# A two-layer hybrid trunk on one core: first stage, latents and side product written in another order, and the delta rule's scratch stored by GpSimd

## The chip, the cores and the metric

The kernel runs on one core of a Trainium2 chip. The time of a run is the device time of that core in microseconds (us). Besides the plain times there is one profiled execution of the kernel, from which all views of the profile come.

## What is computed

Two layers of a trunk over 1024 tokens of width 1024, all in float32. The even layer is a multiscale pool and a differential attention side by side; the odd layer is latent attention (MLA) and a gated delta rule side by side. After each layer a gated side product is added.

```python
def even_layer(h, ...):
    z = h @ w_in
    a_in, a_gate, q, k, v, b_gate = _split(z, EVEN_WIDTHS)
    a = multiscale_pool(a_in)            # trailing-window mean minus the token
    a = (a @ pool_w) * pool_scale * silu(a_gate)
    q, k = partial_rope(rmsnorm(q)), partial_rope(rmsnorm(k))
    o = diff_attention(q, k, v, lam)     # two softmaxes, second one times lam
    o = rmsnorm(o) * silu(b_gate)
    return concat([a, o]) @ w_out

def odd_layer(h, ...):
    cq, ckv, k_rope, c_gate, qkv, d_b, d_a, d_gate = _split(h @ w_in, ODD_WIDTHS)
    q = rmsnorm(cq) @ w_uq;  kv = rmsnorm(ckv) @ w_ukv
    oc = causal_attention(rope(rmsnorm(q)), rope(rmsnorm(k)), v_c) * silu(c_gate)
    dq, dk, dv = silu(causal_depthwise_conv(qkv))
    beta = sigmoid(d_b);  g = -exp(a_log) * softplus(d_a + dt_bias)
    od = gated_delta_rule(l2norm(dq), l2norm(dk), dv, g, beta)   # chunks of 64
    od = rmsnorm(od) * silu(d_gate)
    return concat([oc, od]) @ w_out

for i in range(2):
    h = h + (even_layer, odd_layer)[i](rmsnorm(h, norm_g[i]), ...)
    h = h + sigmoid(h @ ple_w_gate[i]) * (p[i] @ ple_w_proj[i])
```

## The kernel before

**Matrix products.** Every large product is made in float32r with both operands split into a high and a low part, three matmuls for one (`mm3`, L142 to L144). `split` makes the parts: ScalarE copies the high part (L134), VectorE subtracts (L135). `wload` loads 128 rows of a weight into one of four `raw` buffers by a transfer that SP issues (L158), and splits it into one of nine `hi` and nine `lo` slots. `proj_T` makes a transposed block of 128 features by 512 tokens, 24 matmuls at eight rows of weights; `proj_tok` a block of 128 tokens. Results stand in eight PSUM banks: two `acc`, two `s`, two `x`, one `tr`, one `o`.

**Order.** Each engine executes its own list of instructions in order. A scheduling layer makes the lists from the program, so that code written in one order need not stand so on an engine. Larger pieces are Python generators, and `step(...)` advances them one piece at a time, which lays one piece's matmuls beside another's vector work.

**First stage.** The input arrives in two halves of 512 tokens (`load_x`), each split per row block k. The first half makes four column blocks of the pool's input in `first`. The second makes three in `second`, and the fourth (`proj_T`, j = 3) after all k, so that the nine weight slots are held until then. `finish_x` turns the sums of squares into a reciprocal root per token (`token_rstd`, L182; `token_row`, L190). `pool_in` scales the columns to the pool's input (L347, L350, L352). `even_pool(b)` makes window sums by shifted additions on GpSimd (L421), finishes them on VectorE (L431 to L433) and multiplies by `pool_w` (L437). `even_proj` makes a head's q, k, v and gate; its L463 reads a gate from the product's bank.

**Heads and filler.** Six heads of attention follow, `even_attn(hd)` beside `even_proj(hd + 1)`; beside head 5 runs `ple_proj(0)`, the first side product (`pT` times `ple_w_proj`, stored at L595). `out_stage` ends a layer; at the end of layer 0 it sums the squares of its result (L687) for the next normalization.

**Odd layer.** `latent` makes, for each of eight blocks of 128 tokens, a block z (24 matmuls of 456 columns), normalizes it (L771), transposes it (L774) through the one `tr` bank and splits it. `decay` makes the delta rule's gates (L852 to L870). `mla_qkv` makes queries, keys and values per token block, with the weights of `latent_weights` (L788). `gdn_qkv` and `gdn_prep` make, for each of four heads and two halves, six scratch arrays of 128 x 512 and store them to DRAM: q (L899), kw and kd (L952), vb (L957), L and QK (L968). `block_load` reads L back in another layout (L980) and `block_solve` inverts all the diagonal blocks at once on VectorE (L994, L996). `mla_prep` makes K and Q for attention (L1144 to L1146, reading `zq`). `ple_proj(1)` makes the second side product beside that. `gdn_solve` builds the inverse U from the solved blocks (L1010, transposed at L1020 to L1022, matmuls from L1027), then the scan and the MLA attention run beside each other, and `out_stage` ends the layer.

## Time and profile before

| | |
|---|---|
| median of three runs | 1472.44 us (1470.59 to 1477.74) |
| the profiled execution | 1472.82 us |
| its span | 1471.1 us |
| mean clock granted to TensorE | 0.993 of full speed |
| TensorE busy | 1415.7 us, 96% of the span |
| the one queue of transfers (all issued by SP) | 39.7% of what 16 DMA engines could take |

The span is the time from the first to the last recorded instruction. PE is TensorE, DVE VectorE, ACT ScalarE, POOL GpSimd; SP's queue is written SPq. A row of the timeline gives start, duration, engine, line, operation, output and inputs, and in square brackets the idle time of the engine just before it with what ended that. A row of a stretch gives its length and busy time of each engine, then the clock that was granted, the share of the DMA engines and GB/s.

The page's chain of work that ended last holds 3% of TensorE and nothing else of weight; it is the end of `out_stage` of layer 1, which the diff does not touch. So the views that matter are those by stretch and by wait.

### The profile page before, as it was taken

How to read it: one execution, taken by the hardware profiler on the slowest of the kernel's cores; microseconds unless marked ns; L12 is line 12 of the kernel's file. 1: busy time of each engine (PE TensorE's matmuls, PEld its weight loads, DVE VectorE, ACT ScalarE, POOL GpSimd, SP SyncE). 2: the span in 40 equal slices, each digit the busy share in tenths (PEclk: the TensorE clock that was granted, in tenths of full speed). 3: DMA queues.
4: the chain of work that ended last, by engine and by line, in shares of the span. 5: the costliest groups of instructions: out<-in, count | busy, mean ns of one | idle time of the engine just before them, and what ended most of it. 6: DMA issues, size and time to landing. Idle time of an engine off the chain costs nothing. (4 is left out here: it accounts for less than half of the span.)

```text
span 1471.1 us, 22586 instructions
## 1 busy us (share of the span) xinstructions
PE 1415.7 (96%) x7447; PEld 1153.8 (78%) x7447; DVE 977.9 (66%) x2853; ACT 664.6 (45%) x1662; POOL 195.9 (13%) x341
## 2 busy tenths in 40 slices
PE   8999999999999999999999999999989999999998
PEld 6677888888887778887777878778768888887876
DVE  6756766666667785366676788997557887633342
ACT  6335555565656732343554543434334455722220
POOL 0321101111011000022015621210000000000021
PEclk9999999999999999999999999999999999999999
DMA  6223424232333563333424433343676634443332
GB/s 225 61 70 103 108 51 108 51 108 51 101 101 99 160 200 109 108 121 119 103 70 165 181 107 102 99 134 110 214 250 195 204 124 135 129 137 104 126 108 86
DMA packets 127605, 181.51 MB, mean 123 GB/s; under 512 B 28393, under 2 KB 55297, under 8 KB 127489
## 3 DMA queue, kind: packets, MB, share of 16 engines
q1 hardware_dynamic: 127488, 180.08, 39.7%
q8 instruction: 59, 0.97, 0.3%
q14 instruction: 58, 0.47, 0.1%
HBM read 108.20 MB, written 52.95 MB: 110 GB/s over the span
## 5 line engine op out<-in xcount | busy, mean ns | idle before, releaser
L143 PE MATMUL acc<-wl,x 128*128 128x512 f32 (+1 forms) x576 | 229.5, 399 | 3.2 <-DVE wl L135 3.2
L142 PE MATMUL acc<-wh,x 128*128 128x512 f32 (+1 forms) x576 | 231.0, 402 | 0.7 <-DVE g L463 0.6
L144 PE MATMUL acc<-wh,x 128*128 128x512 f32 (+1 forms) x576 | 228.0, 396 | 0.0
L142 PE MATMUL acc<-x,wh 128*128 128x512 f32 x504 | 202.9, 403 | 6.1 <-ACT wh L134 4.6
L144 PE MATMUL acc<-x,wl 128*128 128x512 f32 x504 | 200.2, 399 | 3.6 <-DVE wl L135 3.3
L143 PE MATMUL acc<-x,wh 128*128 128x512 f32 x504 | 199.8, 397 | 0.0
L135 DVE TENSOR_TENSOR wl<-raw,wh 128x512 fp32r<-128x512 f32 (+2 forms) x184 | 124.5, 698 | 31.8 <-ACT wh L134 30.2
L134 ACT CAST wh<-raw 128x512 fp32r<-128x512 f32 (+2 forms) x184 | 105.9, 600 | 69.4 <-PE acc L143 22.6
L143 PEld LDWEIGHTS acc<-wl,x 128*128 128x128 f32 x576 | 109.2, 190 | 26.9 <-DVE wl L135 4.2
L142 PEld LDWEIGHTS acc<-wh,x 128*128 128x128 f32 x576 | 109.2, 190 | 24.4 <-DVE g L463 1.4
L144 PEld LDWEIGHTS acc<-wh,x 128*128 128x128 f32 x576 | 109.0, 189 | 22.5
L142 PEld LDWEIGHTS acc<-x,wh 128*128 128x128 f32 x504 | 94.9, 188 | 29.5 <-ACT wh L134 6.1
L144 PEld LDWEIGHTS acc<-x,wl 128*128 128x128 f32 x504 | 94.8, 188 | 29.5 <-DVE wl L135 7.4
L261 ACT ACTIVATE p<-p,mx 128x128 f32<-128x128 f32 (+7 forms) x128 | 99.4, 777 | 33.7 <-DVE mx L257 23.2
L143 PEld LDWEIGHTS acc<-x,wh 128*128 128x128 f32 x504 | 95.1, 189 | 21.6 <-issue 0.2
L674 POOL TENSOR_TENSOR u<-hp,hp 128x512 f32<-128x512 f32 x32 | 43.2, 1350 | 473.4 <-DVE hp L135 190.8
L144 PE MATMUL acc<-hp,wl 128*128 128x512 f32 x256 | 101.6, 397 | 0.6 <-DVE wl L135 0.6
L143 PE MATMUL acc<-hp,wh 128*128 128x512 f32 x256 | 101.6, 397 | 0.0
L142 PE MATMUL acc<-hp,wh 128*128 128x512 f32 x256 | 101.5, 396 | 0.0
L257 DVE CUSTOM_DVE_ANT_0 p<-s,cst 128x512 f32<-128x512 f32 (+3 forms) x128 | 74.2, 586 | 26.8 <-PE s L532 15.6
L672 DVE SCALAR_TENSOR_TENSOR th<-th,ld 128x512 f32<-128x512 f32 x32 | 30.0, 937 | 75.7 <-ACT th L670 75.7
L459 ACT ACTIVATE z<-acc,rstd 128x256 f32<-128x256 f32 x48 | 22.8, 475 | 101.3 <-PE acc L144 99.1
(554 smaller groups left out, 2866.4 us busy)
## 6 DMA issues: line engine op xcount, KB each, us to landing
raw<-in_ev_w_in SPq DMA_DIRECT2D x56, 256.0 KB
Q<-sq SPq DMA_DIRECT2D x96, 128.0 KB
qkv<-zz SPq DMA_DIRECT2D x16, 640.0 KB
raw<-cat SPq DMA_DIRECT2D x32, 256.0 KB
raw<-in_ple_w_gate SPq DMA_DIRECT2D x32, 256.0 KB
ld<-ple SPq DMA_DIRECT2D x32, 256.0 KB
zq<-qkv SPq DMA_DIRECT2D x16, 512.0 KB
K<-sq SPq DMA_DIRECT2D x48, 128.0 KB
```

What stands on the lines that cost most here:

```text
L134: s.copy(hi, src)
L135: v.tensor_tensor(out=lo, in0=src, in1=hi.bitcast(F32), op=ALU.subtract)
L142: pe.matmul(ps, lh, rh, start=first, stop=False)
L143: pe.matmul(ps, lh, rl, start=False, stop=False)
L144: pe.matmul(ps, ll, rh, start=False, stop=last)
L257: v.tensor_tensor_reduce(out=pm[:, c * 512:c * 512 + n], in0=ps[:, 0:n], in1=mk, scale=-scale, scalar=prev, op0=ALU.add, op1=ALU.min, accu ...
L261: s.activation(pm[:, 0:w], pm[:, 0:w], AF.Exp, bias=prev, scale=-1.0, accum_out=sums)
L459: s.activation(z[:, t % 4, :], ps[:, 0:256], AF.Identity, scale=rstd[0][:, t:t + 1])
L672: v.scalar_tensor_tensor(out=th, in0=th, scalar=1.0, in1=r, op0=ALU.add, op1=ALU.mult)
L674: g.tensor_tensor(out=u, in0=hi.bitcast(F32), in1=lo.bitcast(F32), op=ALU.add)
```

## The change

The change has eight parts.

1. *First stage.* Both halves make all four columns per k (`pool_ps`); the second half has the banks `x`, `x`, `tr`, `o`. Two results of the first half are copied to SBUF by ScalarE, so that the `acc` banks come free. Squares are taken one k behind (`square_x`). `finish_x` uses the banks `acc` and `s`.
2. *Lambda* is made later, after the first step of the pool.
3. *Pool and projection.* `even_pool` is a generator with a pause before its matmuls, and the steps alternate with `even_proj(0)`.
4. *Side product.* `ple_proj` loads the weights of both column halves ahead of its first pause, and head 5 has a longer list of steps.
5. *Sums of layer 0.* The first half's normalization is made after two blocks of the second half.
6. *Latents.* The transposes of a block are written one block later; `latent_weights` is written ahead of the rope, `decay` after two token blocks of `mla_qkv`.
7. *Scratch stores.* The 48 stores of q, kw, kd, vb, L and QK are issued by GpSimd (`g.dma_start`) instead of SP.
8. *`gdn_solve`.* Its copies and negations go from VectorE to ScalarE.

```diff
+    for h in range(2):
+        for k in range(KC):
+            load_x(h, k)
+            if h == 0:
+                w_pool += wload(a["ev_w_in"], 0, 512, row=k, nk=1)
+            if k:
+                square_x(h, k - 1, sums[h])
+            for j in range(4):
+                q = slice(j * P, j * P + P)
+                mm3(pool_ps[h][j], w_pool[k][0][:, q], w_pool[k][1][:, q], *hn[k][h], k == 0, k == KC - 1)
...
-    second.append(bank("acc"))
-    proj_T(hn, w_pool, 3, 1, second[3])
...
+        yield
         for h in range(2):
             pm = bank("s")
             pe.matmul(pm, pw[:, b, :], x[:, 16 + 512 * h:528 + 512 * h], start=True, stop=True)
...
+        w = [wload(a["ple_w_proj"][layer], 512 * gq, 512, nk=2) for gq in range(2)]
         yield
         for gq in range(2):
-            w = wload(a["ple_w_proj"][layer], 512 * gq, 512, nk=2)
...
-    step(ahead)
-    even_pool(0)
-    step(ahead)
-    even_pool(1)
-    step(ahead, ahead)
+    pools_ = [even_pool(b) for b in range(2)]
+    step(pools_[0], ahead)
...
+    step(ahead, pools_[0], pools_[1], ahead, ahead, pools_[1])
...
+        if hd < 5:
+            step(at, at, ahead, late, done, at, at, ahead, at, at, ahead, at, ahead, at, at)
+        else:
+            step(at, at, ahead, ahead, late, done, at, ahead, at, at, ahead, at, ahead, at, ahead, at, ahead, at, ahead)
...
-                if more and gq == 1:
-                    set_rstd(1, h, token_rstd(sums[h]))
+                    if more and gq == h == 1 and j == 1:
+                        set_rstd(1, 0, token_rstd(sums[0]))
+        if more:
+            set_rstd(1, 1, token_rstd(sums[1]))
...
+            zs.append(z)
+            if c:
+                transposes(c - 1)
+        transposes(3)
...
+    we = latent_weights()
     krt = T("gz", 2, pool=bp).rearrange("p (t o d) -> p t o d", o=1, d=64)
     rope(g, kr.unsqueeze(2), krt, cos1, sin1, 1, 32)
-    decay()
-    we = latent_weights()
...
     qkvs, gp0, gp1 = both(), gate_proj(0), gate_proj(1)
-    for _ in range(NT):
+    for t in range(NT):
         step(qkvs, gp0, qkvs)
+        if t == 1:
+            decay()
...
-            dma.dma_start(gsc[n][hd][h], dst)
+            g.dma_start(gsc[n][hd][h], dst)
...
-        v.tensor_copy(W[32:64], ps[32:64, 0:P])
-        v.tensor_copy(W[96:128], ps[96:128, 0:P])
+        s.copy(W[32:64], ps[32:64, 0:P])
+        s.copy(W[96:128], ps[96:128, 0:P])
...
-        v.tensor_scalar(U3[0:64, :, 64:128], c3(px[0:64, 0:256]), -1.0, None, ALU.mult)
+        s.activation(U3[0:64, :, 64:128], c3(px[0:64, 0:256]), AF.Identity, scale=-1.0)
```

Line numbers below that belong to the changed kernel lie about 17 higher than before in the odd layer, and 4 or 5 lower from the even projections to the latents (L463 is L459 there, L774 is L769; L870 is L887, L1027 is L1044).

**VectorE around the end of the first stage.** Before, in this order (`wl` are weights of the products, `Q` and `p` the pool's inputs, `g_785` the gate of the first product block, whose bank the third block needs):

```order
L135 TENSOR_TENSOR wl_779<-raw_777,wh_778 128x512
L207 TENSOR_TENSOR g_628<-g_628 128x64
L212 TENSOR_SCALAR g_628<-g_628 128x64
L431 TENSOR_TENSOR p_847<-p_847,cst 128x16
L433 SCALAR_TENSOR_TENSOR p_180<-p_847,cst,p_180 128x1008
L213 SCALAR_TENSOR_TENSOR pt_629<-g_628 128x64
L432 TENSOR_TENSOR p_180<-p_847,p_180 128x16
L135 TENSOR_TENSOR wl_1228<-raw_1226,wh_1227 128x512
L215 COPY pt_630<-pt_629 128x64
L212 TENSOR_SCALAR g_628<-g_628 128x64
L463 SCALAR_TENSOR_TENSOR g_785<-th_812,acc_786 128x128
```

Now:

```order
L352 TENSOR_TENSOR Q_182<-o_192,g_169 128x512
L203 TENSOR_SCALAR g_630<-cst,npos 128x8 x3
L426 TENSOR_TENSOR p_729<-p_729,cst 128x16
L428 SCALAR_TENSOR_TENSOR p_180<-p_729,cst,p_180 128x1008
L354 SCALAR_TENSOR_TENSOR Q_182<-z_622,Q_182 128x512
L354 SCALAR_TENSOR_TENSOR Q_182<-z_626,Q_182 128x512
L206 TENSOR_SCALAR g_630<-g_630 128x64
L427 TENSOR_TENSOR p_180<-p_729,p_180 128x16
L207 TENSOR_TENSOR g_630<-g_630 128x64
L212 TENSOR_SCALAR g_630<-g_630 128x64
L459 SCALAR_TENSOR_TENSOR g_789<-th_816,acc_790 128x128
```

The weights' splits have left this place for earlier ones. The pool's L426, which reads GpSimd's sums, now stands ahead of both additions into Q and of the gate.

**ScalarE in the first latents.** Before (`z` are latents split out of the transpose bank `tr`, `ea` the decay's exponential, whose `alog` is loaded by SP):

```order
L760 ACTIVATE gz_7844<-acc_7819,rstd_148 128x456
L762 ACTIVATE nx_7845,lss_7847<-gz_7844 128x256
L763 ACTIVATE nx_7845,lss_7847<-gz_7844 128x128
L764 ACTIVATE nx_7845,sskr<-gz_7844 128x64
L134 CAST z_7756<-tr_7809 128x128
L870 ACTIVATE ea_8293<-alog 128x4
L134 CAST z_7757<-tr_7809 128x128
```

Now:

```order
L779 ACTIVATE gz_7836<-acc_7811,rstd_148 128x456
L781 ACTIVATE nx_7837,lss_7839<-gz_7836 128x256
L782 ACTIVATE nx_7837,lss_7839<-gz_7836 128x128
L783 ACTIVATE nx_7837,sskr<-gz_7836 128x64
L134 CAST z_7758<-tr_7861 128x128
L887 ACTIVATE ea_8587<-alog 128x4
L134 CAST z_7759<-tr_7861 128x128
```

The decay is written later in the program, but this operation stands where it stood, between two casts out of the bank.

**SP around the second side product.** Before (`raw` are weights of the second column half, `ple` results, `xinv` the solved blocks, `U` their loads):

```order
L595 DMA ple_3_0_121<-ple_11569 128x512
L158 DMA raw_11588<-in_ple_w_proj 128x512
L595 DMA ple_3_1_122<-ple_11579 128x512
L158 DMA raw_11594<-in_ple_w_proj 128x512
L997 DMA xinv<-nx_11207 128x1024
L1007 DMA L_11805<-gL_0_7660 128x512
L1012 DMA vb_11813<-gvb_0_7652 128x512
L1013 DMA kw_11814<-gkw_0_7636 128x512
L1010 DMA U_11702<-xinv 32x4x32
L595 DMA ple_4_0_123<-ple_11601 128x512
```

Now the four weight loads stand together ahead of the first `zq`, and at this place there is:

```order
L591 DMA ple_3_1_122<-ple_11593 128x512
L1014 DMA xinv<-nx_11233 128x1024
L591 DMA ple_4_0_123<-ple_11603 128x512
L591 DMA ple_4_1_124<-ple_11613 128x512
L591 DMA ple_5_0_125<-ple_11623 128x512
L1027 DMA U_11704<-xinv 32x4x32
L591 DMA ple_5_1_126<-ple_11633 128x512
L1027 DMA U_11704<-xinv 32x4x32
L591 DMA ple_6_0_127<-ple_11643 128x512
L1027 DMA U_11704<-xinv 32x4x32 x2
```

The weight loads are gone from here, and the last two loads of U stand behind the store of the thirteenth result.

## The prediction

> **What bounds the kernel now.** I read the page's list of busy times first, then the busy times of stretches, then what TensorE waited for.

> ```profile
> PE 1415.7 (96%) x7447; PEld 1153.8 (78%) x7447; DVE 977.9 (66%) x2853; ACT 664.6 (45%) x1662; POOL 195.9 (13%) x341
> ...
> core 0: us, PE busy (x) PEld busy (x) DVE busy (x) ACT busy (x) POOL busy (x), PEclk, DMA share, GB/s
> 0.00:100.00 100.00, 89.68 (x365) 69.31 (x366) 71.36 (x180) 44.30 (x80) 20.34 (x39) 0.98 0.35 116
> 440.00:540.00 100.00, 92.08 (x486) 74.20 (x485) 73.98 (x222) 62.04 (x146) 5.46 (x9) 0.98 0.53 163
> 540.00:680.00 140.00, 140.00 (x601) 112.63 (x600) 80.20 (x136) 45.66 (x75) 16.65 (x15) 1.00 0.35 114
> 680.00:800.00 120.00, 111.48 (x514) 91.56 (x513) 80.65 (x305) 57.35 (x201) 28.47 (x63) 0.99 0.35 100
> 840.00:1000.00 160.00, 151.76 (x731) 121.42 (x730) 141.86 (x316) 63.62 (x188) 34.98 (x49) 1.00 0.34 112
> 1040.00:1100.00 60.00, 52.24 (x277) 41.74 (x275) 37.94 (x116) 20.52 (x39) 1.03 (x3) 0.91 0.68 226
> 1100.00:1280.00 180.00, 175.51 (x1537) 152.35 (x1536) 141.99 (x576) 94.81 (x209) 5.04 (x12) 1.00 0.51 156
> ```

> TensorE bounds the whole: it is busy in 1415.7 of 1471.1 us. The change takes no matmul away, so it can win only from the 55.4 us in which TensorE stands still and from the stretches in which its granted clock is below 1.00. The idle time is length less busy time: 10.3 us in the first 100, 7.9 in 440 to 540, 8.5 in 680 to 800, 8.2 in 840 to 1000, 7.8 in 1040 to 1100 and 4.5 in 1100 to 1280. A clock of 0.91 over 60 us is another 5.4 us at most. The stretch 540 to 680 is saturated and gives the price of a 512-column matmul: 140.00 / 601 = 0.233 us.

> ```profile
> PE acc L142 <- ACT wh L134: 8.8, 3, 4.2
> PE acc L143 <- DVE wl L135: 3.2, 1, 3.2
> PE s L1144 <- DMA zq<-qkv: 3.1, 1, 3.1
> PE x L921 <- DVE sp L966: 2.7, 2, 1.5
> PE tr L774 <- DVE z L135: 1.9, 1, 1.9
> PE tr L774 <- DVE gz L771: 1.6, 5, 0.5
> PE x L143 <- DVE nx L135: 1.6, 1, 1.6
> PE o L182 <- DVE sums L687: 1.6, 2, 1.0
> ```

> Columns: total us, times, longest. Each wait is small, so each part of the change is priced at its own wait.

> **First stage, 0 to 100 us.** Timeline rows of four engines (start, us, engine, line; in brackets the idle time before it and what ended it):

> ```profile
> 51.24 2.72 ACT L134 CAST wh<-raw 128x512 fp32r<-128x512 f32 x4 [4.42 <-PE acc L143]
> 58.44 1.92 POOL L421 TENSOR_TENSOR p<-p 128x1039 f32<-128x1039 f32 x1 [28.30 <-DVE p L347]
> 60.62 2.41 POOL L421 TENSOR_TENSOR p<-p 64x1038 f32<-64x1038 f32 x1
> 63.10 2.25 POOL L421 TENSOR_TENSOR p<-Q 128x1039 f32<-128x1039 f32 x1
> 62.01 3.89 DVE L352 SCALAR_TENSOR_TENSOR Q<-z,Q 128x512 f32<-128x512 f32 x2 [0.76 <-ACT z L351]
> 66.85 1.26 DVE L433 SCALAR_TENSOR_TENSOR p<-p,cst,p 128x1008 f32<-128x1008 f32 x1
> 66.66 0.50 PE L143 MATMUL acc<-wl,x 128*128 128x512 f32 x1 [3.15 <-DVE wl L135]
> 68.64 0.63 PE L142 MATMUL acc<-wh,x 128*128 128x512 f32 x1
> 73.44 1.88 PE L437 MATMUL s<-p,pw 128*128 128x512 f32 x4
> ```

> Before, ScalarE waits 4.42 us for TensorE, because all nine weight slots are held until the fourth column of the second half is done. The last splits come late, and one stands behind two VectorE operations that take 3.89 us beside GpSimd's shifted sums. TensorE waits 3.15 us and then runs slow for a while (0.63 us a record where 0.40 is usual; the clock of 0.98 over 100 us bounds that by 2 us, I count 1.7): 4.9 in all. With four columns per k the slots come free with the block, and this goes.

> What is late next: the third product block (acc_859) needs the bank that g_789 (L459) still reads, and g_789 now stands on VectorE behind the pool's L426 and L428. TensorE would be at acc_859 where it now is at 73.44, less 4.9: 68.5. The pool's sums start 19 matmuls later (so many product matmuls stand ahead of the second row product now), 4.4 us, so those that end at 63.0 end at 67.4. From there to g_789 VectorE has L428's 1.26 us, two additions of half its size (0.7 each, an estimate from it) and some 0.8 of small ones: ready at 70.9 alone, or up to 4 later beside GpSimd's next sums (2.25 and more). The wait is 2.4 to 6.4 us; I take 3.5, with 0.8 for half a chance of the slow clock and 0.6 at the next blocks, where the same chain comes round. Against 4.9: **0** (-4 to +3).

> **Filler of head 5, 440 to 540 us.**

> ```profile
> 516.74 0.50 PE L142 MATMUL acc<-x,wh 128*128 128x512 f32 x1 [1.00 <-DVE z L129]
> 520.23 1.02 PE L562 MATMUL tr<-cst,o 128*128 128x128 f32 x4 [0.43 <-DVE o L555]
> ```

> The side product is spread more thinly over head 5, so its weights and the first output products lie between these waits. The two waits are 1.4 us, with their restarts 2; the rope wait and its slow clock at 469 stay. **2** (0 to 5, the upper end all that is not ordinary attention).

> **Latents, 680 to 800 us.** The second half's transposes now stand one block of 24 matmuls behind their z. At 456 columns a block is 24 x 0.208 = 5.0 us (0.233 x 456/512), where the chain needs 18 matmuls and 0.5, 4.2 us: five waits, 1.6 us, go, with 0.4 of restart. The reduction of the first half's sums moves back by more than 30 matmuls, and of L182's 1.6 us about 1.2 go. The decay is written later, but its exponential stands in ScalarE's order where it stood.

> ```profile
> 722.84 0.21 ACT L870 ACTIVATE ea<-alog 128x4 f32<-128x4 f32 x1 [2.60 <-DMA alog<-in_od_a_log]
> ```

> It blocks the casts that free the one transpose bank, so the 1.9 us wait at L774 and its slow clock stay. So does nx at 1.6: rope runs on GpSimd beside it as before. With 0.8 for the decay's other operations: **4** (2 to 7).

> **Scratch stores by GpSimd, 840 to 1000 us.** All 48 stores (q, kw, kd, vb, L, QK; four heads, two halves) leave SP's queue.

> ```profile
> SPq L968 <- DVE sp L966: 40.0, 14, 6.1
> ...
> 922.45 0.32 SPq L968 DMA_DIRECT2D gL<-sp  x1
> 922.86 1.35 SPq L158 DMA_DIRECT2D raw<-in_od_w_in  x3
> 924.63 0.49 ACT L134 CAST wh<-raw 128x384 fp32r<-128x384 f32 x1
> ...
> L674 POOL TENSOR_TENSOR u<-hp,hp 128x512 f32<-128x512 f32 x32 | 43.2, 1350 | 473.4 <-DVE hp L135 190.8
> ```

> Now a store that waits for VectorE holds SP, the next head's weight loads stand behind it, and ScalarE's split of them follows: the second and third of the L142 waits (8.8 less 4.2) belong here. SP's new order has up to two heads' loads ahead of the next block load, so I count 4.6 as gone. The price is on GpSimd: its gate products and masks are queued behind stores that wait for VectorE, and the trace holds no transfer that GpSimd issues. One costs it between SP's 0.32 us and its own 128x512 operation's 1.35 us; nearest in kind is the 0.32, so I take it: 48 x 0.32 = 15.4 us of an engine busy 35.0 of 160. VectorE is busy 141.9 of 160, and what slows it there is paid; I take off 2.6 for it. **2** (-8 to +6).

> [...]

> **Delta rule's inverse and the second side product, 1040 to 1100 us.**

> ```profile
> 1063.88 0.40 PE L142 MATMUL acc<-pT,wh 128*128 128x512 f32 x1
> ...
> 1078.95 0.33 SPq L158 DMA_DIRECT2D raw<-in_ple_w_proj  x1
> 1080.77 0.80 PE L142 MATMUL acc<-pT,wh 128*128 128x512 f32 x1 [4.19 <-ACT wh L134]
> 1083.43 0.32 SPq L1010 DMA_DIRECT2D U<-xinv  x1
> 1086.29 0.48 DVE L1020 STREAM_TRANSPOSE wk<-U 32x32 f32<-32x32 f32 x4 [2.81 <-DMA U<-xinv]
> 1094.96 0.21 PE L1027 MATMUL acc<-wk,L 32*32 32x32 f32 x1
> ```

> Before, the second half's weights are loaded at 1078.95, when slots come free, and TensorE waits 4.19 us and runs slow after it. Now both halves' weights are loaded ahead. The 16 blocks of six matmuls start at 1063.88, take 96 x 0.233 = 22.4 us and end at 1086.3; the solve could start at 1087. What is late next: its U loads. The last two stand behind the store of the thirteenth block, 1063.88 + 13 x 1.40 + 0.8 = 1082.9; with 0.8 to issue, 2.86 to land (1083.43 to 1086.29) and a transpose or two of 0.48, the solve starts at 1087.9 for 1094.96. Taken with a us for the longer wait of SP ahead of them: **6** (3 to 7.5). The zq wait of 3.1 stays; its buffers are the same.

> **Solve's copies to ScalarE, 1100 to 1280 us.** Ten small operations per solve, eight solves, leave VectorE (142.0 of 180) for ScalarE (94.8). Both have room; of 4.5 us idle I take **0.5** (0 to 3).

> **Sum.** 0 + 2 + 4 + 2 + 6 + 0.5 = 14.5 us. The profiled execution took 1472.8 us (span 1471.1), 0.4 over the median of the three, so 1458.3: **1458 us**. The upper ends give 31.5 us, 1441; the lower ends (-4, 0, 2, -8, 3, 0) give -7, 1480.

> **Rivals.**
> 1. *The stalls only move* (0.23). At acc_859 the wait is 6 us with the slow clock, and GpSimd's queue gives back what the loads win. For it speaks the 3.89 us row. -4 + 1 + 2 - 3 + 4 = 0: about 1473, 1466 to 1480.
> 2. *GpSimd's stores hold VectorE up* (0.09, slower). [...]
> 3. *SP set free helps more* (0.13). All 8.2 us idle of the preparation go (6 more than taken), the first stage wins 3 and the latents 7: 1458 - 6 - 3 - 3 = 1446, 1441 to 1450.

> **Numbers.** Forecast 0.55 (1450 to 1465), rivals as given. Range 1442 to 1480: it leaves out rival 2 and a corner of rival 3. A measurement can tell about 0.5%, 7 us, from no change: faster (under 1465) 0.55 + 0.13, slower (over 1480) 0.10, the rest 0.22.

> **What would show it.** Right: no wait of 3 us at L142 near 1076; a new wait near 68 for g (L459); the wait for z at the first latents still there; SP without long waits for sp; the solve near 1080 (1087.9 less the 8 us of the parts before it). Wrong: VectorE's busy time per operation in the preparation up by more than a tenth, or block loads landing later than the weights they stand ahead of.

## The result, and the profile after

Twelve runs of the changed kernel have a median of 1464.9 us (1461.3 to 1469.3), twelve of the kernel before beside them 1471.9 (1469.9 to 1477.7). The ratio is 0.9945, with a 95% interval from 0.9933 to 0.9957. The change wins 7.0 us where 14.5 were forecast: the direction holds, and the time lies in the range, at the upper edge of the band from 1450 to 1465 that had most of the weight. One run of e7 (2279.8 us, at a granted clock of 0.557) and one of the kernel before (1949.7 us, 0.655) were slow and are left out below. The profiled execution has a span of 1463.3 us against 1471.1 before.

The page's busy times and queues, and the same stretches as before (columns as there):

```profile
PE 1413.0 (97%) x7447; PEld 1155.3 (79%) x7447; DVE 959.2 (66%) x2797; ACT 682.5 (47%) x1720; POOL 216.3 (15%) x389
q1 hardware_dynamic: 120576, 167.49, 38.0%
q0 software_dynamic: 3840, 12.59, 2.3%
...
0.00:100.00 100.00, 89.30 (x362) 69.63 (x363) 69.23 (x178) 46.09 (x84) 19.25 (x39) 0.97 0.35 111
440.00:540.00 100.00, 91.04 (x486) 73.72 (x485) 73.63 (x223) 61.06 (x146) 5.46 (x9) 0.98 0.52 158
680.00:800.00 120.00, 115.17 (x537) 96.58 (x536) 84.44 (x315) 60.30 (x216) 32.75 (x74) 0.99 0.38 111
840.00:1000.00 160.00, 153.28 (x735) 123.72 (x734) 143.35 (x312) 63.58 (x188) 49.07 (x81) 0.99 0.33 110
1000.00:1040.00 40.00, 38.09 (x179) 31.00 (x178) 25.21 (x61) 15.40 (x38) 6.71 (x12) 0.96 0.49 161
1040.00:1100.00 60.00, 56.20 (x360) 45.40 (x360) 36.91 (x119) 25.58 (x57) 1.86 (x5) 0.97 0.73 232
```

What to see: the latents (680 to 800) gained busy time, 115.17 us of 120 against 111.48. The second side product (1040 to 1100) gained 4 us of it and 0.06 of clock. The first 100 us and head 5 gained nothing. A second queue has appeared, the one that GpSimd issues.

What TensorE waited for (total us, times, longest):

```profile
PE x L938 <- DVE sp L983: 8.0, 8, 1.7
PE acc L142 <- ACT wh L134: 3.7, 3, 2.7
PE s L1160 <- DVE Q L1162: 3.1, 1, 3.1
PE acc L142 <- DVE g L459: 3.0, 1, 3.0
PE acc L142 <- DVE t L661: 2.9, 2, 2.5
```

The waits for `wh` (ScalarE's part of the weights) fell from 8.8 to 3.7 us. In their place stand a wait for the gate g, one for t, and three times as much waiting for sp: 8.0 us where it was 2.7.

**Where the 8 us came from.** Stretches by the clock shift as work moves, so I compare at equal work. Every matmul of a trace is weighted with the usual time of its shape, and I ask when each kernel has done the work that the kernel before had done at a given time. The table holds the gain in us (all from profiled executions), with the median of all runs and the ratio to the kernel before beside it. The runs are described below.

| run | 440 | 545 | 842 | 1040 | 1084 | 1283 | median us (runs) | ratio, 95% |
|---|---|---|---|---|---|---|---|---|
| changed kernel | -1.4 | -1.4 | 4.2 | 0.4 | 5.6 | 8.3 | 1464.9 (12) | 0.9945 [0.9933, 0.9957] |
| e1 stores by SP | -2.6 | -0.8 | 5.0 | 5.0 | 7.8 | 6.1 | 1461.9 (4) | 0.9946 [0.9928, 0.9963] |
| e2 before, stores by GpSimd | -1.1 | 0.3 | 3.7 | 1.7 | 3.7 | 1.9 | 1471.8 (10) | 1.0006 [0.9996, 1.0015] |
| e3 kw's stores by SP | -2.3 | -3.1 | 2.8 | -3.8 | 1.2 | 4.1 | 1465.3 (10) | 0.9973 [0.9957, 0.9989] |
| e4 first stage as before | 1.0 | 2.2 | 7.8 | 4.6 | 9.9 | 13.9 | 1460.2 (4) | 0.9925 [0.9910, 0.9940] |
| e5 steps of head 5 as before | -1.9 | -1.1 | 4.6 | 0.4 | 5.4 | 4.9 | 1463.0 (10) | 0.9952 [0.9938, 0.9966] |
| e6 gate copied | -3.0 | -3.9 | 1.8 | -1.9 | 3.3 | 6.8 | 1466.2 (8) | 0.9959 [0.9944, 0.9973] |
| e7 before, weights early | -0.2 | 0.9 | 2.5 | 2.6 | 5.5 | 5.0 | 1466.1 (9) | 0.9970 [0.9958, 0.9982] |
| e8 first stage and stores as before | 0.5 | 3.8 | 7.3 | 7.3 | 9.8 | 13.7 | 1460.1 (4) | 0.9928 [0.9903, 0.9953] |
| e9 own buffer | -1.0 | 2.3 | 8.7 | 5.8 | 10.5 | 13.4 | 1461.8 (6) | 0.9937 [0.9923, 0.9952] |
| e10 own buffer, stores by SP | -1.1 | 1.7 | 5.8 | 4.9 | 7.4 | 10.2 | 1461.2 (5) | 0.9926 [0.9913, 0.9939] |
| e11 loads early | -1.7 | 1.1 | 7.1 | 3.4 | 8.5 | 11.3 | 1462.0 (4) | 0.9940 [0.9928, 0.9953] |
| e12 three edits | -2.3 | -2.6 | 3.9 | 1.1 | 6.8 | 10.8 | 1463.0 (6) | 0.9943 [0.9925, 0.9961] |

In the first row the stages read: first stage -1.4, head 5 0, latents +5.6, delta rule's preparation -3.8, side product and inverse +5.2, the rest +2.7 by 1283. Single executions differ by a few half-clock periods of 1.7 us (last section), so differences of 2 us between rows need the medians too; those of e1 and e5 have three such periods in a row near 1173 us, which the other runs lack.

The kernel before is one execution too, and it had a half-clock period at 726.85 us that e2 and e7, whose latents are the same, do not have. They gain 3.4 and 1.6 us between 545 and 842 without any change there. The eleven runs with the new latents gain 3.5 to 6.5, 5.5 in the mean. The new latents are thus worth nearer 4 us than 5.6. Between 1084 and 1283 the runs with the new solve gain 2.7 to 4.0, e1 and e5 apart, where e2 and e7 lose 1.8 and 0.5. Between 842 and 1040 the eight runs with all stores on GpSimd lose 2.0 to 4.2, the five with all on SP between 0.9 and nothing.

### The profile page after: what moved, and what is told of

Its sections match the earlier page's. It is cut to its first block, busy times and chain, and to the rows that moved or that the text cites. A ratio compares the mean times of both kernels' runs of the same rounds, so it can differ in the third digit from the quotient of the medians.

```text
span 1463.3 us, 22639 instructions
## 1 busy us (share of the span) xinstructions
PE 1413.0 (97%) x7447; PEld 1155.3 (79%) x7447; DVE 959.2 (66%) x2797; ACT 682.5 (47%) x1720; POOL 216.3 (15%) x389
## 5 line engine op out<-in xcount | busy, mean ns | idle before, releaser
L142 PE MATMUL acc<-wh,x 128*128 128x512 f32 (+1 forms) x576 | 233.3, 405 | 3.0 <-DVE g L459 3.0
L143 PE MATMUL acc<-wl,x 128*128 128x512 f32 (+1 forms) x576 | 230.4, 400 | 0.0
L142 PE MATMUL acc<-x,wh 128*128 128x512 f32 x496 | 200.3, 405 | 6.9 <-ACT wh L134 3.7
L143 PE MATMUL acc<-x,wh 128*128 128x512 f32 x496 | 197.6, 399 | 0.0
L134 ACT CAST wh<-raw 128x512 fp32r<-128x512 f32 (+2 forms) x184 | 106.0, 600 | 69.8 <-PE acc L143 19.0
L135 DVE TENSOR_TENSOR wl<-raw,wh 128x512 fp32r<-128x512 f32 (+2 forms) x184 | 118.8, 668 | 28.5 <-ACT wh L134 25.6
L142 PEld LDWEIGHTS acc<-wh,x 128*128 128x128 f32 x576 | 109.8, 191 | 26.6 <-DVE g L459 3.5
L143 PEld LDWEIGHTS acc<-wl,x 128*128 128x128 f32 x576 | 110.1, 191 | 22.8 <-issue 0.7
L142 PEld LDWEIGHTS acc<-x,wh 128*128 128x128 f32 x496 | 94.1, 190 | 29.7 <-ACT wh L134 4.4
L143 PEld LDWEIGHTS acc<-x,wh 128*128 128x128 f32 x496 | 94.4, 190 | 21.2
L142 PE MATMUL acc<-hp,wh 128*128 128x512 f32 x256 | 101.5, 397 | 0.0
L143 PE MATMUL acc<-hp,wh 128*128 128x512 f32 x256 | 101.5, 396 | 0.0
L455 ACT ACTIVATE z<-acc,rstd 128x256 f32<-128x256 f32 x48 | 22.8, 475 | 95.7 <-PE acc L144 91.9
```

Source lines behind the costliest of these rows:

```text
L134: s.copy(hi, src)
L135: v.tensor_tensor(out=lo, in0=src, in1=hi.bitcast(F32), op=ALU.subtract)
L142: pe.matmul(ps, lh, rh, start=first, stop=False)
L143: pe.matmul(ps, lh, rl, start=False, stop=False)
L455: s.activation(z[:, t % 4, :], ps[:, 0:256], AF.Identity, scale=rstd[0][:, t:t + 1])
```

## Experiments on the scratch stores

**e1**: all stores back on SP. **e2**: the kernel before, with nothing but these stores on GpSimd. **e3**: the changed kernel with kw's stores alone on SP.

```diff
# e1 (at all four places); e2 the reverse in the kernel before
-            g.dma_start(gsc[n][hd][h], dst)
+            dma.dma_start(gsc[n][hd][h], dst)
# e3
-            g.dma_start(gsc[n][hd][h], dst)
+            (dma if n == "kw" else g).dma_start(gsc[n][hd][h], dst)
```

> The changed kernel with all 48 scratch stores issued by SP again. Theory A (GpSimd's gate products, L945, stand behind its store of kw, start when VectorE has just made kw, and so run beside VectorE's small chain of L954 to L962 that the next transposes wait for): the eight waits of the transposes L938 for L983, 8.0 us in the changed kernel, fall to 3 or less, L954 falls from 1.2 us to about 0.2, and the stretch 840 to 1040 gives back some 3 us: about 1461. Rival B (the stores themselves do not matter, VectorE is full in that stretch whoever stores): waits and time as in the changed kernel, 1464 to 1466. Rival C (SP's freed queue was worth its 4.6 us of weight waits): those come back, 1467 to 1469.

> The kernel before with nothing changed but the 48 stores issued by GpSimd. Theory A: waits for weights of about 4.6 us go and waits of the transposes for VectorE of 5 to 8 us come, 1472 to 1475. Rival B: no change, 1471 to 1473. Rival C: 1467 to 1469.

> The changed kernel with only the eight stores of kw issued by SP, so that GpSimd's gate products no longer stand behind a store of kw. Theory A: as with all stores on SP, L954 falls to about 0.2 us and the time to about 1461 to 1462. Rival D (transfers that GpSimd issues land late and hold the block loads up): 40 stores are still there, time and waits of SP for gL (79.6 us) as in the changed kernel, 1464 to 1466.

What GpSimd paid: its transfer rows by line between 840 and 1040 us in the changed kernel (busy us, mean ns, idle before), and two rows of the list of transfers, with the median time to landing (us) last:

```profile
L969 POOL DMA_DIRECT2D gkw<-sp x8 | 4.3, 540 | 31.4 <-DVE sp L968 31.4
...
gkw<-sp POOLq DMA_DIRECT2D x8, 256.0 KB, 3.8
gL<-sp POOLq DMA_DIRECT2D x8, 256.0 KB, 2.3
```

A store costs GpSimd 0.54 us (the six arrays 0.54 to 0.59), between the 0.32 and 1.35 us of the prediction. GpSimd waits 31.4 us for VectorE's sp in front of kw's stores. What is queued behind them comes late, the gate products L945, and these now fall on VectorE's chain of small operations. Timeline of the changed kernel, GpSimd and VectorE, then VectorE's row at the same place in e1:

```profile
992.16 0.54 POOL L969 DMA_DIRECT2D gkw<-sp  x1 [2.99 <-DVE sp L968]
992.71 1.05 POOL L945 TENSOR_TENSOR w<-cst,gdh 128x512 fp32r<-128x512 f32 x1
993.71 1.05 POOL L945 TENSOR_TENSOR w<-cst,gdl 128x512 fp32r<-128x512 f32 x1
992.44 2.36 DVE L954 TENSOR_SCALAR gm<-gm 128x8 f32<-128x8 f32 x1
```

```profile
991.40 0.17 DVE L954 TENSOR_SCALAR gm<-gm 128x8 f32<-128x8 f32 x1
```

An operation on 128 x 8 numbers took 2.36 us here and ended when both products had ended; beside no product, in e1, it took 0.17. The store itself added less than 0.1 us: three of the eight, at 859.63, 904.66 and 948.60 us, ran beside a store of kw without a product and took 0.23 to 0.25. The group of eight, by line, in the changed kernel, e1, e2 and e3 (one row each):

```profile
L954 DVE TENSOR_SCALAR gm<-gm 128x8 f32<-128x8 f32 x8 | 8.7, 1085 | 0.3 <-ACT sqj L940 0.3
```

```profile
L954 DVE TENSOR_SCALAR gm<-gm 128x8 f32<-128x8 f32 x8 | 1.3, 163 | 0.4 <-ACT sqj L940 0.4
```

```profile
L937 DVE TENSOR_SCALAR gm<-gm 128x8 f32<-128x8 f32 x8 | 10.6, 1320 | 0.3 <-ACT sqj L923 0.3
```

```profile
L954 DVE TENSOR_SCALAR gm<-gm 128x8 f32<-128x8 f32 x8 | 1.6, 195 | 0.0
```

The mean follows the place of kw's stores in all four. What it does to TensorE, in the waits between 840 and 1040 us: before, then e1 and e3. The changed kernel has the 8.0 us shown above, all of them in this stretch.

```profile
PE acc L144 <- DVE wl L135: 3.1, 5, 1.1
PE x L921 <- DVE sp L966: 2.7, 2, 1.5
PE acc L142 <- ACT wh L134: 1.6, 1, 1.6
```

```profile
PE x L938 <- DVE sp L983: 2.8, 2, 1.4
PE acc L144 <- DVE wl L135: 2.0, 4, 0.9
PE acc L142 <- ACT wh L134: 1.6, 1, 1.6
```

```profile
PE x L938 <- DVE sp L983: 4.9, 3, 1.7
PE acc L144 <- DVE wl L135: 4.4, 2, 2.2
```

The 4.7 us of waits for weights (3.1 + 1.6) are gone with the stores on GpSimd. But the waits for sp rise by 5.3 us, and two half-clock periods (877 and 1010 us) add 3.4. That is 4.7 - 5.3 - 3.4 = -4.0, for -3.8 in the table. In e1 the waits for sp are 2.8 us and the stage loses nothing (5.0 to 5.0), as its theory A has it. e8 against e4, the same difference in another kernel, is 7.3 to 7.3 against 7.8 to 4.6. e2 loses 2.0 in the stage with this part alone: it has the same waits for sp (8.4 us), but no half-clock period in the stage. These are the waits of its theory A, with the time of its rival B (1471.8 us). e3 shows the limit of the idea: the small operation is quick again and the waits for sp fall to 4.9, but SP's queue now holds weight loads behind kw's stores (4.4 us of waits for weights), two half-clock stretches of 6.8 us stand beside these waits (923 and 971 us), and the stage loses 6.6. Its time of 1465.3 us is not the 1461 to 1462 that was expected; only the small operation did as expected.

Yet the ratios of e1 and the changed kernel, of e8 and e4, and of e10 and e9 agree within their intervals. What SP's stores save by 1040 they give back at 1050. Rows of TensorE there, the changed kernel, e1 and e7:

```profile
1054.84 1.09 PE L1160 MATMUL s<-cst,zq 128*128 128x128 f32 x4 [3.09 <-DVE Q L1162]
```

```profile
1051.80 0.80 PE L142 MATMUL acc<-wh,x 128*128 128x512 f32 x1 [4.64 <-DVE gz L927]
```

```profile
1054.28 0.79 PE L142 MATMUL acc<-wh,x 128*128 128x512 f32 x1 [4.64 <-DVE gz L910]
```

The wait is 1.5 us longer in e1, and two half-clock periods follow instead of one. e8 and e10 have the same wait (4.64 and 4.58 us), and so has e7, the kernel before with the side product's weights loaded early. The kernel before has 3.07 us there, for zq. So the longer wait comes where early weight loads and the stores are both on SP; which of SP's transfers makes gz late was not followed. The stores on GpSimd lose their stage, spare the early loads this wait, and are worth nothing in the whole that these runs can tell; e2's ratio of 1.0006 says the same of them alone.

## Experiments on the first stage

**e4** has the first stage, lambda and the pool's steps as before, **e8** the stores too. **e6** lets ScalarE copy the gate of the first two token blocks, **e9** gives the second half's tanh a buffer that is free, **e10** is e9 with e1's stores. **e12** is e6, e9 and e11 (below) together.

```diff
# e4, cut to its core
-    pool_ps = [[bank(n) for n in tags] for tags in (("acc", "acc", "s", "s"), ("x", "x", "tr", "o"))]
+    second = [bank(n) for n in ("x", "x", "tr")]
...
-    step(pools_[0], ahead)
+    step(ahead)
+    even_pool(0)
# e6, in even_proj (L459), with early=True for head 0
+                gate = ps[:, 384:512]
+                if early and t2 == 0:
+                    gate = gg[:, cc]
+                    s.copy(gate, ps[:, 384:512])
-                ... in0=th, scalar=1.0, in1=ps[:, 384:512], ...
+                ... in0=th, scalar=1.0, in1=gate, ...
# e9, in pool_in (L351)
-        ag, th = pg[2 * (j - 2) + h], T("z", 2)
+        ag, th = pg[2 * (j - 2) + h], (slots[0][j - 2] if h else T("z", 2))
```

> The changed kernel with the first stage, lambda and the steps of pool and first projection as before; all the rest changed. If the new first stage costs what the traces of the two kernels show at the first attention (1.4 us behind): 1463 to 1464, with the 3.15 us wait for wl at L143 back. If its loss is made up later (waits of the first heads that would come anyway): 1464 to 1466.

> The changed kernel with the first stage, lambda and the pool's steps as before and all 48 stores issued by SP; filler, latents, side product's weights and the solve's copies as changed. If the two parts taken back cost what they cost apart (4.7 and 3.0 us by medians): 1457. If they overlap: 1460 to 1462.

> The changed kernel; for the first two token blocks of the first projection ScalarE copies the gate out of the product's bank, and VectorE reads the copy, so that the bank no longer waits for VectorE's L459 behind the pool. Two copies of 128x128 are added on ScalarE. Theory (the wait of 3.0 us at 72.3 and the 6.8 us of half clock after it are that operation's): both go, the first attention starts 4 to 6 us earlier than in the changed kernel, 1459 to 1461. Rival (the next block waits for VectorE in the same way): 1 to 2 us, 1463 to 1464.

> The changed kernel with one edit: the tanh of the second half's pool gate (th in pool_in, h = 1) is written into a K buffer that the first half has done with, instead of a buffer of tag z. Theory A (the wait of 3.0 us at 73.16 and the half clock behind it come from the buffer: L455's z_787 takes the buffer of th, which VectorE's L354 reads last, and L354 stands behind the pool's L428 beside GpSimd): the row ACT L455 no longer waits for L354, TensorE's 3.0 us wait for g goes, with it the 6.8 us of half clock near 73 (3.4 us of work): the gain over before at 116 us rises from -1.3 to about +3, and the median falls from 1464.9 to about 1461. Rival B (the gate itself, L459 on VectorE behind the pool, is what holds the bank): ACT L455 moves but the wait at L142 for g stays at 2 us or more, median within 1 us of 1464.9. Rival C (the stall only moves to the pool's matmuls or the next blocks): gain at 116 unchanged though the wait at 73 is gone.

> The changed kernel with the own buffer for the gate's tanh and all 48 scratch stores on SP again. If the two losses were independent and additive, 1464.9 - 4 (first stage) - 3 (stores, as the run with stores on SP showed: 1461.9) = about 1458. If they overlap, as the run with first stage and stores both undone showed against the one with the first stage alone (1460.1 and 1460.2), it is no faster than the run with the own buffer alone: about 1460 to 1461.

> The changed kernel with three edits together: the second half's tanh in a K buffer of its own, the gate of the first two token blocks copied out of the bank by ScalarE, and the second half's loads in out_stage written earlier. Theory A (the first stage's new wait has two causes in series, the buffer that holds L455 and the gate L459 behind the pool's L426 and L428; each of the single edits left the other): now the 2.6 to 3.0 us wait for g near 72 and its half clock go, the gain over before at 116 us is +3 to +4 (it was -0.9 with the buffer alone, -2.2 with the copy alone), median 1457 to 1460. Rival B (the blocks behind wait for the same VectorE chain in any case, so that the stall only moves to 80 to 116 us): no wait near 72, but the gain at 116 stays below +1, median 1461 to 1463.

The new first stage costs some 2 us: the five executions that have it unedited (changed kernel, e1, e3, e5, e11) stand at -1.4 to -2.6 at 440 us, the five that have the old one (before, e2, e4, e7, e8) at -1.1 to 1.0. Without it (e4) the median is 1460.2 against 1464.9, lower than was expected, but the intervals of the two ratios overlap. e6, e9 and e12 ask what holds TensorE there. Timeline rows of the changed kernel: three of VectorE, then ScalarE, then TensorE.

```profile
67.34 2.94 DVE L428 SCALAR_TENSOR_TENSOR p<-p,cst,p 128x1008 f32<-128x1008 f32 x1
70.20 1.28 DVE L354 SCALAR_TENSOR_TENSOR Q<-z,Q 128x512 f32<-128x512 f32 x2
71.99 0.29 DVE L459 SCALAR_TENSOR_TENSOR g<-th,acc 128x128 f32<-128x128 f32 x1
70.97 0.47 ACT L455 ACTIVATE z<-acc,rstd 128x256 f32<-128x256 f32 x1 [3.80 <-DVE Q L354]
72.34 0.80 PE L142 MATMUL acc<-wh,x 128*128 128x512 f32 x1 [3.03 <-DVE g L459]
```

L428 takes 2.94 us beside GpSimd's next sums (1.26 alone, at 66.85 us in the kernel before), both L354 and the gate stand behind it, and ScalarE's z needs the buffer that L354 reads. In e6, where ScalarE copies the gate, the wait stayed (2.84 us), because ScalarE itself still waited 3.80 us for L354. In e9 ScalarE is free, and now the gate alone holds the bank (rows of e9):

```profile
63.37 0.48 ACT L455 ACTIVATE z<-acc,rstd 128x256 f32<-128x256 f32 x1 [1.51 <-PE acc L144]
71.21 0.27 DVE L459 SCALAR_TENSOR_TENSOR g<-th,acc 128x128 f32<-128x128 f32 x1
71.53 0.79 PE L142 MATMUL acc<-wh,x 128*128 128x512 f32 x1 [2.60 <-DVE g L459]
```

With both edits, e12, the wait near 72 is gone, and the gain is 4.7 us at the work of 79 us. At that of 90 it is 0.4: the wait has moved to the third gate, which is not copied and stands on VectorE behind 37 other operations from 72 us on, 32 of them those of the rope tables. Three of these took 1.79 to 2.38 us, where others like them took 0.18 to 0.23; in the changed kernel three took 1.61 to 2.46 us beside GpSimd's sums (72.20 to 78.36 us). Rows of e12:

```profile
76.44 2.38 DVE L213 SCALAR_TENSOR_TENSOR pt<-g 128x64 f32<-128x64 f32 x1
85.78 0.28 DVE L463 SCALAR_TENSOR_TENSOR g<-th,acc 128x128 f32<-128x128 f32 x1
86.11 0.51 PE L142 MATMUL acc<-wh,x 128*128 128x512 f32 x1 [3.51 <-DVE g L463]
```

So rival B of e12 holds: VectorE's chain from the pool to the rope tables sets when the third bank is free (the gate is written at 85.78 us in e12, at 85.05 in the changed kernel), and what TensorE wins ahead of that, it waits there. The kernel before came to that block late, after its 3.15 us wait, and waited only 0.57. A version that spreads the rope tables out was not tried. The times of e6 (1466.2 us) and e9 (1461.8) do not fit the waits: e6 lies above both of its expectations, and e9 came out as fast as its theory A said although the wait of 2.60 us stayed. With an interval that overlaps the changed kernel's, e9 shows no sure gain in time.

## Experiments on head 5 and the second side product

**e5** has head 5's list of steps as before. **e11** writes the second half's loads in `out_stage` two product blocks earlier. **e7** is the kernel before with part 4's weight loads alone.

```diff
# e5
-        if hd < 5:
-            step(at, at, ahead, late, done, at, at, ahead, at, at, ahead, at, ahead, at, at)
-        else:
-            step(at, at, ahead, ahead, late, done, at, ahead, at, at, ahead, at, ahead, at, ahead, at, ahead, at, ahead)
+        step(at, at, ahead, late, done, at, at, ahead, at, at, ahead, at, ahead, at, at)
# e7, in ple_proj
+        w = [wload(a["ple_w_proj"][layer], 512 * gq, 512, nk=2) for gq in range(2)]
         yield
         for gq in range(2):
-            w = wload(a["ple_w_proj"][layer], 512 * gq, 512, nk=2)
# e11, in out_stage
-                if gq == 0 and h == 1:
-                    load_cat(1)
...
+                    if gq == h == 0 and j == 1:
+                        load_cat(1)
```

> The changed kernel with the list of steps of head 5 as before (the side product's weights still ahead). Theory: what the longer list wins by 530 (2.6 us ahead in the changed kernel's trace) is lost at the first sums of the layer's output, which wait for the last head's way through DRAM (2.5 us and a slow clock after it at 531 to 536), so the list is worth nothing: 1464 to 1466, and at 545 as far from the kernel before as the changed kernel is, within 1 us. Rival (the list does win its 2 us): 1467 to 1469.

> The changed kernel with one edit: in out_stage the second half's loads of the concatenated heads are written after the second product block of the first half instead of after the fourth. Theory A (the filler's gain is lost at 534 because VectorE's L661, which frees the bank, stands behind the splits of the second half's loads): the 2.5 us wait at L142 for t near 534 and its half clock go, the gain over before at 545 rises from -1.4 to about +3, median about 1461. Rival B (the wait is the load of the residual ld or the store and load of the last head through DRAM, which SP issues in turn): the wait stays or takes another name, median within 1 us of 1464.9 or above.

> The kernel before with nothing changed but the weights of both side products loaded ahead of their first block. Theory (the wait of 4.19 us near 1076 and the slow clock behind it are those loads'): the wait goes and 5 to 6 us are won between 1060 and 1100: 1465 to 1467. Rival (without the other parts the solve's loads of U are late next): 1468 to 1470.

Head 5: in this pair the list is worth nothing (-1.1 at 545 us without it, -1.4 with it). The changed kernel has a gain of 2.6 us at the work of 530, which goes at one wait and the half-clock period behind it (535.92 us). Its rows on VectorE and TensorE:

```profile
533.72 0.69 DVE L661 TENSOR_TENSOR t<-acc,ld 128x512 f32<-128x512 f32 x1 [0.93 <-DMA ld<-in_xT]
534.47 0.50 PE L142 MATMUL acc<-x,wh 128*128 128x512 f32 x1 [2.55 <-DVE t L661]
```

In e11 the wait is still there, 2.23 us, for the load of the residual (`ld`): rival B by the wait, though its median of 1462.0 lies nearer theory A. It gained at 545 all the same, but by a half-clock period that did not follow, which this edit was not shown to cause: e8, e9 and e10, without the edit, wait 1.25 to 2.42 us there, no half clock follows either, and they gain 2.8 to 3.3 us between 440 and 545, where e5 gains 0.8. So what the list wins is kept or lost with that period. e5's median of 1463.0 fits neither of its expectations.

The side product: e7 gains 5.8 us between the work of 1075 (-0.3) and of 1084 us (5.5) with its loads alone, as the changed kernel does (-0.2 to 5.6). But e7 loses 2.9 us ahead of that, between 1040 (2.6) and 1075, at the wait of 4.64 us shown above; the changed kernel, with its stores on GpSimd, loses 0.6. In the whole e7 wins 0.3%, some 4 us, as was expected.

## Why the prediction was near, and where it was off

By its own terms, forecast against the gain at equal work:

| term | forecast | measured | |
|---|---|---|---|
| first stage | 0 (-4 to 3) | -1.4 | in its bounds |
| head 5 | 2 (0 to 5) | 0 | at the lower end |
| latents | 4 (2 to 7) | 5.6 | in its bounds |
| stores by GpSimd | 2 (-8 to 6) | -3.8 | wrong sign |
| side product and inverse | 6 (3 to 7.5) | 5.2 | as forecast |
| solve's copies, and the rest | 0.5 (0 to 3) | 2.4 at 1440 us | in its bounds |
| sum | 14.5 | 8.0 | |

The forecast was near partly by luck. Head 5 and the stores fell 7.8 us short together, the first stage and the side product 2.2 more; the latents and the rest gave back 3.5. The measured terms are of one execution each; the other runs put the latents nearer 4.

- *First stage.* The new wait for g came where it was forecast (2.4 to 6.4 us; 3.03 measured), and for the reason given, L428 beside GpSimd. The buffer behind ScalarE's z and the rope tables were not seen. The half clock was under-priced: 6.8 us at half speed cost 3.4, where 0.8 was taken (in e1, e3, e5 and e11 it was one period, 1.7).
- *Head 5.* The waits near 516 and 520 us went. The step "what is late next" was left out here, and the residual's load was next.
- *Latents.* That the transposes' wait for z would stay was right. The changed kernel's own trace does not have it, but nine of the eleven runs with the new latents do, 0.85 to 1.97 us long, as in this row of waits of e9:

```profile
PE tr L769 <- DVE z L135: 1.3, 1, 1.3
```

In the two that lack it (the changed kernel and e3) a half-clock period stands just ahead, at 713.41 and 715.26 us; whether that is the reason was not tested. The half clock at 727 is missing from e2 and e7 as well, so its absence cannot be put down to the change. The forecast of 4 is what the comparison of all runs gives; the 5.6 of the table holds some luck. This part and the solve's copies were not run alone.
- *Stores.* The gain of 4.6 us on weights came out (4.7), but by luck. The two waits for `wh` that the prediction counted here are the 1.6 us at 925 and this one, at the start of the kernel, which stays (2.74 us in the changed kernel):

```profile
6.79 1.22 PE L142 MATMUL acc<-x,wh 128*128 128x512 f32 x2 [3.00 <-ACT wh L134]
```

What went in its place are 3.1 us of waits for `wl`. The step that failed is "what slows it there is paid; I take off 2.6 for it": the waits for sp rose by 5.3 us and the clock cost 3.4. That stores would be cheap on GpSimd held (0.54 us). What was missed is that waiting in front of them moves GpSimd's products onto VectorE's small chain. SP did not come free either: its block load now waits 79.6 us in all for the landing of gL, where 40.0 us were spent on sp before.
- *Rival 2*, GpSimd's stores that hold VectorE up, fell: between 840 and 1000 us VectorE is busy 143.35 us for 312 operations against 141.86 for 316, 2% more each, and not a tenth; the small operation L954 takes less than 0.1 us more beside a store alone.
- *Landing of the stores.* They landed after 2.3 to 3.8 us (medians of the six arrays), with VectorE busy for 143.35 of the 160 us between 840 and 1000; how long SP's stores took, the traces do not show.
- *Inverse.* The solve was put near 1080, 1087.9 less the 8 us of the parts before it. It starts at 1088.30, 6.7 us earlier than before (1094.96): the step was near, the 8 us before it were not there. Its own terms add up to 1087.0 to 1087.5 and not to 1087.9.
- *Rivals 1 and 3.* Rival 1, stalls that only move, came true for the first stage and for the stores, in part for the side product (e7), and not for the latents; the time lies between it and the forecast. Rival 3 needed the preparation's idle time to go, and there the stage lost.

e4 and e8, at 1460 us, have the lowest medians, without the new first stage; e9 and e10 keep it, with one buffer changed, and their intervals overlap those, and that of the changed kernel too.

## What to carry over

When a wait is taken off the bounding engine, look for the next moment at which that engine needs a result of the engine behind it: if that engine's chain is already full, the wait only moves (72 us to 86 us in e12). A store moved to another engine's queue cost less by its own time (0.54 us) than by what stood behind it there: see where that engine's other operations land, and beside which. Short waits on TensorE should be priced with the clock period that may follow (1.7 us of work, behind the waits of 2.55 us at 534 and of 1.70 us at 877), not by their length alone.

## What the runs showed of the hardware

**The half clock came in whole periods of 3.41 us.** Rows of stretches in the changed kernel, cut at these periods (PE busy second, clock third from the end):

```profile
532.50:535.90 3.40, 1.43 (x6) 1.21 (x7) 2.47 (x6) 1.89 (x4) 0.00 (x0) 1.00 0.78 243
535.90:539.30 3.40, 3.40 (x10) 2.65 (x9) 3.40 (x7) 1.01 (x2) 1.35 (x1) 0.50 0.46 140
873.90:877.30 3.40, 1.47 (x9) 0.79 (x8) 3.40 (x9) 1.88 (x6) 0.64 (x2) 0.99 0.20 77
877.30:880.70 3.40, 3.40 (x11) 2.81 (x10) 2.86 (x6) 2.53 (x14) 2.35 (x5) 0.51 0.48 132
962.60:966.00 3.40, 1.81 (x13) 1.38 (x12) 3.40 (x9) 2.50 (x8) 0.90 (x3) 1.00 0.22 86
966.00:969.40 3.40, 3.39 (x16) 2.46 (x15) 3.40 (x8) 2.25 (x13) 1.25 (x3) 1.00 0.52 125
```

**Some small VectorE operations took longer beside GpSimd's.** A 128 x 8 operation with one input (L954) took 0.16 us alone, the mean of eight in e1, and 2.36 us beside two GpSimd products of 1.05 us each, one behind the other (992.44 us in the changed kernel). It took 2.46 where a third GpSimd operation followed them (925.32). In the same kernel a 128 x 64 operation of the rope tables (L212) took 1.91 us beside GpSimd's sums (73.95), and 0.18 to 0.19 in its eleven other executions.
